# Attention scores and HGRN levels as matmuls of 64 rows for two heads, a layer norm tail with operands in PSUM, and another order of steps

## The chip, the cores and the metric

The kernel runs on one core of one Trainium2 chip. The metric is the device time of one execution in microseconds; a lower time is better. The engines are TensorE (PE), VectorE (DVE), ScalarE (ACT), GpSimd (POOL) and SyncE (SP), which issues most DMAs. PSUM is the memory that matmuls write to, in banks of 512 float32 per partition.

## What is computed

One layer on x of 512 tokens by 1024 features, float32. One projection gives all parts; three mixers work on them; their outputs, gated by silu, are projected back and normalised:

```python
h = x @ w_in[l]
...
o_nsa = nsa_mixer(...)               # 6 heads in 2 groups: compressed, selected and window branch
o_sb = stick_breaking_mixer(sb_q, sb_k, sb_v)                         # 4 heads
o_hg = hgrn2_mixer(hg_q, hg_f, hg_i, lb_all[l])                       # 6 heads
...
mixed = jnp.concatenate([o_nsa * jax.nn.silu(nsa_z), o_sb * jax.nn.silu(sb_z),
                         o_hg.astype(x.dtype) * jax.nn.silu(hg_z)], axis=-1)
x = layer_norm(ALPHA * x + (mixed @ w_out[l]).astype(x.dtype), ln_g[l], ln_b[l])
```

Heads are 64 wide. The scores of a head are its queries times its keys over these 64 features, for the selected and the window branch of the sparse attention (NSA, with a bias by distance) and for stick-breaking; the compressed branch does the same with 31 block keys. HGRN is a gated linear recurrence over time with a decay per feature: `att[t, s] = sum_d q[t,d] k[s,d] exp(b[t,d] - b[s,d])` within a chunk, and a carried state between chunks.

## The kernel before, in words

*Precision.* Operands of the large matmuls are split in two parts of a shorter float32 type (`F32R`): `hi`, a cast by ACT, and `lo`, the rest, by a subtraction on DVE, on POOL or through a DMA that adds (`split` L183, `load_part` from L262, with a choice for each weight group in `SPLITS`). A product takes three passes: hi with hi, hi with lo, lo with hi (`PASSES` L305).

*Projections.* For a group of weight columns, PE multiplies 8 pieces of 128 features with x. Results have the features on the partitions (`feat` L316 and `blocks` L329, 512 columns a matmul) or the tokens (`tiles` with `tok` L345, up to 274 columns). The out-projection is `out_part` (L902, 512 columns, and the addition to y on DVE at L903).

*Scores.* `qstack` (from L350) takes a block of two heads' queries and makes one tile a head, with hi in 64 of the 128 rows and lo in the other 64. `kstack` (from L360) makes two tiles a head: one with the keys' hi part in both halves, one with lo in the half that faces the queries' hi and zeros in the other. Two matmuls over 128 rows (`qk`, L377) then give all three passes for 128 queries by up to 512 keys. Stick-breaking (`sb_head`, from L685) calls it with 128, 256, 384 and 512 keys a head and adds scan, exponentials and a subtraction of its own on DVE and ACT (L696 to L704); the sparse heads (`nsa_probs`, from L652) with 256 keys for the first query tile (both branches at once), and with 256, 384 and 512 for the others, once a branch; `nsa_exp` (L648, L650) adds the bias, finds the extreme and exponentiates. `nsa_cmp` (from L610) uses 12 matmuls of 512 columns over the two groups (L617) for the compressed scores. `pv` (L384 to L402) transposes probabilities on PE and multiplies them with values.

*HGRN.* `hg_pair` (from L776) takes two heads at a time, 64 features each, so that both fill the 128 rows. The 512 tokens are 4 chunks of 128 (`NT`). Within a chunk the matrix `att` is built in 7 levels (`LEVELS`, 64 down to 1): at a level, a block's second half attends to its first half. DVE forms differences of decays, ACT exponentiates, DVE multiplies the queries by the result, one head at a time, into a tile `qz` in which each head's columns are zero in the other head's rows (L806, 64 rows by 256 elements). Four matmuls over 128 rows by 128 columns, in plain float32, make the level's values (L811), and a masked copy on DVE (L820) or copies on ACT (L817) put them into `att`. A matmul in plain float32 leaves two records on PE in the trace. After the levels come transposes and a product with a single output column (L835, L836), the state's products (L843) and the output's (L857, L859).

*Small matmuls of another shape.* `bias_tables` multiplies a one-hot matrix of 33 rows with a table of 6 columns (L473), for the bias by distance.

*The end.* For each of four token tiles `do_end` does the last part of the out-projection, then `norm_stats` (L905 to L922: statistics on DVE at L911 and L913, two small ACT operations at L915 and L916, the shift at L919 or L921) and `norm_apply` (L924 to L936). For tiles 0 to 2, ACT normalises, and DVE (where the tuple `LN_VECTOR` names it) or POOL multiplies by the weight `lng` (L934); POOL adds the bias `lnb` (L935). For tile 3, DVE does two operations that each combine two steps (L929, L930). The last half tile is projected in two pieces of 256 columns.

*What sets the order.* The string `ORDER` names steps one after the other; most steps are generators, and each mention advances one by one `yield`. So the program text is written in that order, and the scheduler of the tile framework places instructions on the engines in order of priority, which follows the program text unless `high_priority` is in force. `BUFS` gives buffers for the pools, `ENGINES` names the engine for some copies and products. An engine takes its instructions strictly in order, and semaphores tell it when an operand is there.

## Time and profile before

| what | value |
|---|---|
| median of 2 runs | 368.16 us (367.69 to 368.63) |
| the profiled execution's own time | 368.77 us |
| its span (first to last instruction) | 366.9 us |
| granted TensorE clock, mean over the span | 0.99 of full speed |
| busy: PE | 343.1 us (94%), 2002 instructions |
| busy: DVE | 276.8 us (75%) |
| busy: ACT | 248.1 us (68%) |
| busy: POOL | 103.8 us (28%) |

Busy time is time in which an engine works on at least one instruction. Weight loads (PEld) are a row of their own beside PE. The durations that the trace gives for single matmuls overlap with their neighbours', because matmuls are pipelined; the distance from one start to the next is the price. A chain of waits follows the end of the program back, at each step to what released the instruction.

### The profile page before, as it was taken

The numbers are of one execution on the slowest core, as the hardware profiler recorded it, in microseconds if no ns is written. First come the engines' busy times: TensorE is split into PE (matmuls) and PEld (weight loads), VectorE is DVE, ScalarE is ACT, GpSimd is POOL, SyncE is SP. The second block draws the span as 40 slices with busy tenths as digits, with TensorE's granted clock in tenths as the row PEclk, the third lists the DMA queues.
The fourth block names the chain that finished last, engine by engine and source line by source line (L and its number), as shares of the span: only waits on it lengthen the run. The fifth ranks groups of instructions, "written<-read, shape, count | busy, mean of one in ns | idle before, by whom it ended". The sixth has DMA issues, their size and how long they took to land.

```text
span 366.9 us, 5871 instructions
## 1 busy us (share of the span) xinstructions
PE 343.1 (94%) x2002; PEld 290.4 (79%) x2002; DVE 276.8 (75%) x628; ACT 248.1 (68%) x559; POOL 103.8 (28%) x145
## 2 busy tenths in 40 slices
PE   7999999999999998998999998999999899999980
PEld 5787899887888876876788997977877777888870
DVE  2769666689699888898876666788999657732796
ACT  3696963728559998785396777688889988731240
POOL 4065560001201111020471332242131604031092
PEclk9999999999999999999999999999999999999995
DMA  7767365250415472051348619500040698961023
GB/s 244 264 230 198 103 187 155 80 138 2 114 59 126 106 181 49 0 134 41 103 137 210 184 33 223 174 29 2 29 107 10 128 250 223 289 179 22 1 88 143
DMA packets 16910, 45.64 MB, mean 124 GB/s; under 512 B 2786, under 2 KB 3298, under 8 KB 16880
## 3 DMA queue, kind: packets, MB, share of 16 engines
q1 hardware_dynamic: 13568, 33.65, 27.5%
q0 software_dynamic: 3312, 11.61, 17.8%
q8 instruction: 16, 0.26, 0.3%
q14 instruction: 14, 0.11, 0.1%
HBM read 37.27 MB, written 2.14 MB: 107 GB/s over the span
## 4 chain that ended last, share of the span: by engine, by line
PE 56%; DVE 14%; ACT 11%; issue 10%; DMA 5%; POOL 3%; SPq 0%; DVEq 0%; POOLq 0%; ACTq 0%
PE pi L329 16%; PE pi L345 11%; PE pi L902 10%; PE pc L402 3%; PE ma L811 3%; DMA lo<-raw 3%; PE ma L377 2%; PE mb L395 2%; PE pi L316 2%; DVE sr L702 2%; DVE qz L806 2%; DMA xt<-xt 2%; ACT hi L273 2%; DVE att L820 1%; ACT pt L650 1%
## 5 line engine op out<-in xcount | busy, mean ns | idle before, releaser
L329 PE MATMUL pi<-xh,hi 128*128 128x512 f32 x160 | 47.8, 406 | 1.8 <-DVE vs L186 1.3
L329 PE MATMUL pi<-xh,lo 128*128 128x512 f32 x160 | 46.5, 396 | 1.4 <-DMA lo<-raw 1.4
L329 PE MATMUL pi<-xl,hi 128*128 128x512 f32 x160 | 46.6, 397 | 0.0
L902 PE MATMUL pi<-hi,mx 128*128 128x512 f32 (+1 forms) x134 | 40.9, 383 | 0.0
L329 PEld LDWEIGHTS pi<-xh,lo 128*128 128x128 f32 x160 | 29.3, 188 | 7.4 <-DMA lo<-raw 2.2
L329 PEld LDWEIGHTS pi<-xh,hi 128*128 128x128 f32 x160 | 28.5, 189 | 7.4 <-DVE vs L186 1.7
L329 PEld LDWEIGHTS pi<-xl,hi 128*128 128x128 f32 x160 | 29.3, 188 | 5.4
L186 DVE TENSOR_TENSOR pl<-mb,ph 128x384 fp32r<-128x384 f32 (+1 forms) x48 | 28.1, 595 | 6.8 <-ACT ph L185 6.3
L345 PE MATMUL pi<-lo,xh 128*128 128x256 f32 (+1 forms) x160 | 27.6, 286 | 1.5 <-DMA lo<-raw 1.3
L345 PE MATMUL pi<-hi,xh 128*128 128x256 f32 (+1 forms) x160 | 28.1, 290 | 0.6 <-DVE vs L186 0.6
L902 PEld LDWEIGHTS pi<-hi,mx 128*128 128x128 f32 x134 | 24.8, 188 | 4.5
L273 ACT CAST hi<-raw 128x1024 fp32r<-128x1024 f32 (+2 forms) x23 | 23.3, 1013 | 7.0 <-PE pi L902 2.8
L680 POOL TENSOR_SCALAR pt<-pt,sm,gates 128x256 f32<-128x256 f32 (+1 forms) x24 | 17.6, 740 | 33.5 <-DVE sm L677 29.3
L345 PE MATMUL pi<-hi,xl 128*128 128x256 f32 (+1 forms) x160 | 26.7, 284 | 0.0
L650 ACT ACTIVATE pt<-pt,mn 128x256 f32<-128x256 f32 (+3 forms) x42 | 24.5, 586 | 2.4 <-DVE mn L648 2.2
L902 PE MATMUL pi<-lo,mx 128*128 128x512 f32 (+1 forms) x67 | 25.8, 385 | 0.0
L185 ACT CAST ph<-mb 128x384 fp32r<-128x384 f32 (+1 forms) x48 | 24.0, 508 | 1.5 <-PE mb L395 1.3
L345 PEld LDWEIGHTS pi<-hi,xh 128*128 128x128 f32 x160 | 23.0, 190 | 1.6 <-DVE vs L186 0.8
L345 PEld LDWEIGHTS pi<-lo,xh 128*128 128x128 f32 x160 | 22.7, 191 | 1.9 <-DMA lo<-raw 1.5
L811 PEld LDWEIGHTS ma<-qz,kz 128*128 128x128 f32 x168 | 20.8, 191 | 3.7 <-ACT kz L795 1.1
L648 DVE CUSTOM_DVE_ANT_0 pt<-ma,nb 128x256 f32<-128x256 f32 (+3 forms) x42 | 21.2, 511 | 3.4 <-PE ma L377 3.3
L811 PE MATMUL ma<-qz,kz 128*128 128x128 f32 x168 | 22.7, 279 | 1.0 <-ACT kz L795 0.4
(269 smaller groups left out, 845.9 us busy)
## 6 DMA issues: line engine op xcount, KB each, us to landing
raw<-w_in SPq DMA_DIRECT2D x28, 512.0 KB, 3.6
lo<-raw POOLq DMA_DIRECT2D x9, 512.0 KB, 5.1
lo<-w_in POOLq DMA_DIRECT2D x6, 512.0 KB, 5.4
raw<-w_out SPq DMA_DIRECT2D x6, 512.0 KB, 5.1
lo<-w_out POOLq DMA_DIRECT2D x5, 512.0 KB, 5.4
y<-x SPq DMA_DIRECT2D x8, 256.0 KB, 4.2
out<-y SPq DMA_DIRECT2D x8, 256.0 KB, 2.0
xt<-xt SPq DMA_DIRECT2D x3, 512.0 KB, 7.2
```

What stands on the lines that cost most here:

```text
L185: nc.scalar.copy(hi, src)
L186: nc.vector.tensor_tensor(out=lo, in0=src, in1=hi.bitcast(F32), op=ALU.subtract)
L273: nc.scalar.copy(hi, raw)
L316: self.nc.tensor.matmul(ps, w[:, c0:c0 + P], self.xpart(x, kt), start=(n == 0 and j == 0), stop=(n == len(parts) - 1 and j == len(js) - 1))
L329: self.nc.tensor.matmul(ps, w[:, b * P:(b + 1) * P], self.xpart(x, kt), start=(n == 0 and j == 0), stop=(n == len(grp) - 1 and j == len(js ...
L345: self.nc.tensor.matmul(ps[:, :w_], self.xpart(x, kt)[:, i * P:(i + 1) * P], w[:, :w_], start=(j == 0), stop=(j == len(js) - 1))
L402: nc.tensor.matmul(acc[:, j * P:], vt[j], t[:, b:b + w], start=(first and j == 0 and t is h), stop=(last and j == 3 and t is l))
L648: nc.vector.tensor_tensor_reduce(out=dst, in0=src, in1=self.nb[h][:, n - 1::-1], scale=1.0, scalar=3e38, op0=ALU.add, op1=ALU.min, accum_o ...
L650: nc.scalar.activation(dst, dst, AF.Exp, bias=mn, scale=-1.0, accum_out=sm)
L680: (nc.gpsimd if i in POOL_TILES else nc.vector).tensor_scalar(out=pts[i], in0=pts[i], scalar1=sm[:, i:i + 1], scalar2=self.gates[:, i, c:c ...
L811: nc.tensor.matmul(ps[:, c * P:(c + 1) * P], kk[:, c * P:(c + 1) * P], qz[:, c, :, :].rearrange("p h t -> p (h t)"), start=True, stop=True)
L902: nc.tensor.matmul(ps, m, w[:, cs], start=(j == 0), stop=(j == len(jobs) - 1))
```

## The change

Scores. `pair` takes the place of `qstack` and `kstack`: it splits a block of two heads into one hi and one lo tile, each with the first head in rows 0 to 63 and the second in rows 64 to 127. `qk` issues three terms, each as one matmul over the upper 64 rows into one bank and one over the lower 64 rows into another bank. `sb_head` becomes `sb_pair` and `nsa_probs` takes a head of each group at once; `cmp_scores` does the compressed scores of both groups in 18 matmuls of 64 rows.

HGRN. The queries of both heads are multiplied in one full-height operation; the level's product is eight matmuls of 64 rows by 64 columns that alternate between the heads, each head in a bank of its own. `HG_STEPS` takes two levels in one step, with a PSUM tile of two banks for them (pool `psl`). The mask is stored four times over.

The end. Weight and bias of the layer norm are copied into PSUM by ACT, and DVE takes its operand from there; `LN_FORM` names engines by tile, half and operation. The statistics and the last application of tile 3 get `high_priority`, the application of tile 2 stands between them. `ORDER`, `BUFS`, `SPLITS` and `ENGINES` have new values.

```diff
 ORDER = (
-    "x Lhf1 Lhq 4*hf1 3*hq Lhi_sv 3*hi_sv Lhi hi_sv p1 hi Lsq hq hi p1 p0 hi 2*p1 const p1 hi 3*p1 sq p1 p0 sq 2*p0 "
...
+    "x Lhf1 4*hf1 3*hq Lhi_sv 2*hi_sv Lhq 2*hi_sv p1 hq Lsq p1 hi Lhi p0 hi const p1 2*sq hi p0 hi sq p1 p0 sk Lsk p0 "
...
-ENGINES = dict(cl='p', e20='v', e21='p', hq='a', hs='v', hv0='v', hv1='a', hv2='a', k1='a', kb0='v', kb1='v',
-    kb2='v', kd0='v', kt='v', mz0='v', mz1='v', mz2='p', mz3='v', mz4='v', nw0='v', nw1='v', nw2='v', q1='p', qs0='p',
-    qs1='p', qs2='p', tmpta='a', tmptb='v', ts='p', z0='v', z1='a', z2='a', z3='v')
+ENGINES = dict(cl='v', e20='v', e21='p', hq='a', hs='v', hv0='v', hv1='a', hv2='a', k1='a', kb0='v', kb1='p',
+    kb2='v', kd0='v', kt='v', mz0='v', mz1='v', mz2='v', mz3='v', mz4='p', nw0='v', nw1='v', nw2='v', q1='p', qs0='v',
+    qs1='p', qs2='v', tmpta='a', tmptb='v', ts='p', z0='v', z1='a', z2='a', z3='v')
...
+LN_FORM = (("pp", "vp"), ("pp", "pp"), ("vp", "vp"), ("s", "s"))
 WARM = 8
 LEVELS = (64, 32, 16, 8, 4, 2, 1)
 PLAIN = 32
+HG_STEPS = ((6, 0), (1, 2), (3, 4), (5,))
...
-    def qstack(self, ps, scale):
-        nc = self.nc
-        res = []
-        for b, o in ((0, 64), (64, 0)):
-            t = self.g2(dt=F32R, s="q")
-            hi, lo, src = t[b:b + 64, :], t[o:o + 64, :], ps[b:b + 64, :]
-            self.split(hi, lo, src, scale)
-            res.append(t)
...
-            self.zero_r(tl[o:o + 64, :], o)
-            src = ps[b:b + 64, :]
-            nc.scalar.copy(th[b:b + 64, :], src)
-            self.copy("kh", th[o:o + 64, :], src)
-            nc.vector.tensor_tensor(out=tl[b:b + 64, :], in0=src, in1=th[b:b + 64, :].bitcast(F32), op=ALU.subtract)
...
-    def qk(self, out, q, i, k):
-
-        lhs = q[:, i * P:(i + 1) * P]
-        for e in range(2):
-            self.nc.tensor.matmul(out, lhs, k[e], start=(e == 0), stop=(e == 1))
+    def pair(self, ps, scale=None, dst=None):
+        hi, lo = dst or (self.g2(dt=F32R, s="qh"), self.g2(dt=F32R, s="ql"))
+        self.split(hi, lo, ps, scale)
+        return hi, lo
+
+    HALVES = (slice(0, 64), slice(64, 128))
+    TERMS = ((0, 0), (0, 1), (1, 0))
+
+    def qk(self, outs, q, i, ks):
+
+        for n, (e, f) in enumerate(self.TERMS):
+            for out, r in zip(outs, self.HALVES):
+                self.nc.tensor.matmul(out, q[e][r, i * P:(i + 1) * P], ks[f][r], start=(n == 0), stop=(n == 2))
...
+    def cmp_scores(self):
...
+        jobs = [(hp, e, f) for e, f in self.TERMS for hp in range(HPG)]
+        for n, (hp, e, f) in enumerate(jobs):
+            for ps, r in zip(pss, self.HALVES):
+                nc.tensor.matmul(ps[0:96, :], self.kc[f][r, 64 - 32 * hp:160 - 32 * hp], self.q[hp][e][r],
+                                 start=(n == 0), stop=(n == len(jobs) - 1))
...
-            ps = self.ps()
-            self.qk(ps[:, :n], q, i, [t[:, branch, 0:n] for t in self.kk[g]])
-            self.nsa_exp(h, ps[:, :n], pts[i], mn[:, i:i + 1], sm[:, i:i + 1])
+            pss = [self.ps() for _ in heads]
+            self.qk([ps[:, :n] for ps in pss], q, i, ks(branch, n))
+            for h, ps, pts, (mn, sm) in zip(heads, pss, all_pts, stats):
+                self.nsa_exp(h, ps[:, :n], pts[i], mn[:, i:i + 1], sm[:, i:i + 1])
...
+            pss = [self.ps("mb") for _ in range(2)]
+            self.qk([ps[:, :n] for ps in pss], self.sq[p], i, [t[:, :n] for t in self.sk[p]])
...
-        for li in (6, *range(6)):
+        for ls in HG_STEPS:
+            ps = self.psl.tile([P, 2, S], F32, tag="ml", name=self.nm("ml"))
+            for n, li in enumerate(ls):
...
-            for h, r in heads:
-                qo = qz[r, :, h, :].rearrange("p c (n l) -> p c n l", l=L)
+                qv = q.rearrange("p (n l) -> p n l", l=2 * L)[:, :, L:2 * L]
+                qz = self.t2((P, 256), s="qz", tag="tq")
+                qo = qz.rearrange("p (n l) -> p n l", l=L)
...
-                    nc.vector.tensor_tensor(out=qo, in0=qv[r, :, :, 1, :], in1=evc[r, :, :, L:2 * L], op=ALU.mult)
+                    nc.scalar.activation(qz, qz, AF.Exp)
+                    nc.vector.tensor_tensor(out=qo, in0=qo, in1=qv, op=ALU.mult)
...
-            ps = self.ps()
-            for c in range(NT):
-                nc.tensor.matmul(ps[:, c * P:(c + 1) * P], kk[:, c * P:(c + 1) * P],
-                                 qz[:, c, :, :].rearrange("p h t -> p (h t)"), start=True, stop=True)
+                for c in range(NT):
+                    for h, r in heads:
+                        nc.tensor.matmul(ps[:, h, n * 256 + c * 64:n * 256 + c * 64 + 64], kk[r, c * P:(c + 1) * P],
+                                         qz[r, c * 64:(c + 1) * 64], start=True, stop=True)
+                pl = ps[:, :, n * 256:n * 256 + 256]
...
-                nc.vector.copy_predicated(att.rearrange("p c h (n k l) -> p (c h) n k l", k=2, l=L)[:, :, :, 1, :],
-                                          m.unsqueeze(1).to_broadcast([P, 8, 64 // L, L]),
-                                          ps.rearrange("p (g n l) -> p g n l", g=8, l=L))
+                    nc.vector.copy_predicated(att.rearrange("p h c (n k l) -> p h (c n) k l", k=2, l=L)[:, :, :, 1, :],
+                                              m.unsqueeze(1).to_broadcast([P, 2, 256 // L, L]),
+                                              pl.rearrange("p h (n l) -> p h n l", l=L))
...
+            m = LN_FORM[i][e]
+            if m == "s":
+                nc.vector.scalar_tensor_tensor(out=y[e], in0=y[e], scalar=nm, in1=self.lngp[e], op0=ALU.add, op1=ALU.mult)
+                nc.vector.scalar_tensor_tensor(out=y[e], in0=y[e], scalar=rs, in1=self.lnbp[e], op0=ALU.mult, op1=ALU.add)
             else:
                 nc.scalar.activation(y[e], y[e], AF.Identity, scale=rs, bias=nm)
-                eng = nc.vector if (i, e) in LN_VECTOR else nc.gpsimd
-                eng.tensor_tensor(out=y[e], in0=y[e], in1=self.lng[e], op=ALU.mult)
-                nc.gpsimd.tensor_tensor(out=y[e], in0=y[e], in1=self.lnb[e], op=ALU.add)
+                for f, g, gp, op in zip(m, (self.lng[e], self.lnb[e]), (self.lngp[e], self.lnbp[e]), (ALU.mult, ALU.add)):
+                    if f == "v":
+                        nc.vector.tensor_tensor(out=y[e], in0=y[e], in1=gp, op=op)
+                    else:
+                        nc.gpsimd.tensor_tensor(out=y[e], in0=y[e], in1=g, op=op)
...
+        self.lngp, self.lnbp = [], []
+        for l, lp in ((self.lng, self.lngp), (self.lnb, self.lnbp)):
+            for t in l:
+                lp.append(self.ps("mb"))
+                nc.scalar.copy(lp[-1], t)
...
-            st[i] = self.norm_stats(i)
-            if i:
+            if i == NT - 1:
+                with self.tc.high_priority():
+                    st[i] = self.norm_stats(i)
                 self.norm_apply(i - 1, *st[i - 1])
-        self.norm_apply(NT - 1, *st[NT - 1])
...
```

How the instructions move on the engines, in three places. The first is PE early in the projections, where HGRN levels stand between them. Before, a pair's levels stand as `L811` (four matmuls over 128 rows), here two levels behind the projection of `hi_574` and `lo_575` (names of the weight parts; `xh` and `xl` are the parts of x):

```order
L345 MATMUL pi_842<-hi_574,xh_128 128x256 x2
L345 MATMUL pi_842<-hi_574,xl_131 128x256 x2
L345 MATMUL pi_842<-hi_574,xl_132 128x256 x2
L345 MATMUL pi_842<-lo_575,xh_127 128x256 x2
L345 MATMUL pi_842<-lo_575,xh_128 128x256 x2
L811 MATMUL ma_876<-qz_390,kz_401 128x128 x4
L811 MATMUL ma_889<-qz_391,kz_402 128x128 x4
L835 MATMUL ma_904<-ident,kd_898 128x128 x3
```

Now each level is `L808`, eight matmuls of 64 rows and 64 columns, and pieces of a projection (`L331` is `blocks`, `L347` is `tok`) stand between levels:

```order
L331 MATMUL pi_461<-xh_133,lo_430 128x512 x2
L331 MATMUL pi_461<-xh_134,lo_430 128x512
L808 MATMUL ml_607<-qz_623,kz_402 128x64 x8
L331 MATMUL pi_461<-xh_134,lo_430 128x512
L808 MATMUL ml_663<-qz_666,kz_403 128x64 x8
L347 MATMUL pi_707<-hi_696,xh_131 128x256 x2
L347 MATMUL pi_707<-hi_696,xh_132 128x256 x2
L347 MATMUL pi_707<-hi_696,xl_135 128x256 x2
L347 MATMUL pi_707<-hi_696,xl_136 128x256
L808 MATMUL ml_663<-qz_682,kz_401 128x64 x8
```

Runs of 64-row matmuls now alternate with the projection's 128-row ones.

The second is PE in the scores of the sparse attention (`kk` are the keys' tiles, `q` or `qh`, `ql` the queries'). Before, two matmuls a query tile (`L377`), between pieces of a projection:

```order
L329 MATMUL pi_2948<-xh_126,hi_2935 128x512 x2
L329 MATMUL pi_2948<-xl_129,hi_2935 128x512
L377 MATMUL ma_2610<-kk_2085,q_1696 128x256
L377 MATMUL ma_2610<-kk_2086,q_1696 128x256
L377 MATMUL ma_2615<-kk_2085,q_1696 128x384
L377 MATMUL ma_2615<-kk_2086,q_1696 128x384
L329 MATMUL pi_2948<-xl_129,hi_2935 128x512
L329 MATMUL pi_2948<-xl_130,hi_2935 128x512
L377 MATMUL ma_2620<-kk_2085,q_1696 128x512
L377 MATMUL ma_2620<-kk_2086,q_1696 128x512
L377 MATMUL ma_2676<-kk_2085,q_1890 128x256
```

Now six matmuls for two heads (`L364`), the two banks in alternation:

```order
L347 MATMUL pi_2845<-hi_2753,xh_132 128x256
L347 MATMUL pi_2845<-hi_2753,xl_135 128x256 x2
L347 MATMUL pi_2845<-hi_2753,xl_136 128x256
L364 MATMUL ma_2665<-kk_2160,qh_1873 128x384
L364 MATMUL ma_2665<-kk_2161,qh_1873 128x384
L364 MATMUL ma_2665<-kk_2160,ql_1874 128x384
L364 MATMUL ma_2676<-kk_2160,qh_1873 128x512
L364 MATMUL ma_2677<-kk_2160,qh_1873 128x512
L364 MATMUL ma_2676<-kk_2161,qh_1873 128x512
L364 MATMUL ma_2677<-kk_2161,qh_1873 128x512
```

Here, too, a run of 64-row matmuls follows 128-row ones of a projection (`L347`).

The third is DVE at the very end (`y` are the output tiles, `ln` the weights of the norm). Before, the two multiplications of tile 2 (`L934`) stand behind the last addition of a matmul (`L903`) or between it and the last statistics (`L911`):

```order
L921 TENSOR_SCALAR nm_4039<-mv_4034,rs_4036 128x1
L911 BN_STATS bn_4082<-y_3777 128x6
L903 SCALAR_TENSOR_TENSOR y_3873<-y_3873,pi_4060 128x256
L911 BN_STATS bn_4082<-y_3777 128x6
L911 BN_STATS bn_4082<-y_3873 128x6
L903 SCALAR_TENSOR_TENSOR y_3873<-y_3873,pi_4071 128x256
L934 TENSOR_TENSOR y_3758<-y_3758,ln_3892 128x512
L911 BN_STATS bn_4082<-y_3873 128x6
L934 TENSOR_TENSOR y_3854<-y_3854,ln_3894 128x512
L913 BN_AGGR mv_4087<-bn_4082 128x2
L919 TENSOR_SCALAR nm_4092<-mv_4087 128x1
L929 SCALAR_TENSOR_TENSOR y_3777<-y_3777,nm_4092,ln_3892 128x512
```

Now the addition is `L901`, the statistics `L909` and `L911`, and the operands `mb` of the multiplications and of the last operations (`L928`, `L929`) are the copies in PSUM:

```order
L919 TENSOR_SCALAR nm_4161<-mv_4156,rs_4158 128x1
L909 BN_STATS bn_4204<-y_3948 128x6 x2
L901 SCALAR_TENSOR_TENSOR y_3986<-y_3986,pi_4182 128x256
L934 TENSOR_TENSOR y_3872<-y_3872,mb_4013 128x512
L909 BN_STATS bn_4204<-y_3986 128x6
L901 SCALAR_TENSOR_TENSOR y_3986<-y_3986,pi_4193 128x256
L934 TENSOR_TENSOR y_3967<-y_3967,mb_4015 128x512
L909 BN_STATS bn_4204<-y_3986 128x6
L911 BN_AGGR mv_4209<-bn_4204 128x2
L917 TENSOR_SCALAR nm_4214<-mv_4209 128x1
L928 SCALAR_TENSOR_TENSOR y_3948<-y_3948,nm_4214,mb_4013 128x512
L928 SCALAR_TENSOR_TENSOR y_3986<-y_3986,nm_4214,mb_4015 128x512
```

One multiplication and one statistic stand ahead of the last addition.

## Rows read from the trace of the kernel before

**Rows 1.** The page's first part: the span, and TensorE, VectorE, ScalarE, GpSimd.

```profile
span 366.9 us, 5871 instructions
...
PE 343.1 (94%) x2002; PEld 290.4 (79%) x2002; DVE 276.8 (75%) x628; ACT 248.1 (68%) x559; POOL 103.8 (28%) x145
```

**Rows 2.** Busy time by stage: each engine's us (count), PE clock, DMA share, GB/s.

```profile
70.00:170.00 100.00, 94.98 (x574) 80.29 (x573) 87.24 (x188) 73.06 (x170) 13.46 (x21) 1.00 0.38 94
70.00:320.00 250.00, 239.70 (x1435) 201.96 (x1434) 201.95 (x498) 189.56 (x449) 59.94 (x84) 1.00 0.44 115
320.00:356.50 36.50, 36.43 (x170) 30.34 (x168) 20.48 (x37) 12.11 (x21) 12.97 (x11) 1.00 0.29 79
356.50:367.00 10.50, 0.00 (x0) 0.00 (x0) 7.32 (x10) 0.68 (x3) 3.60 (x3) 0.63 0.34 126
```

**Rows 3.** Chain of waits, whole span: its shares by line.

```profile
PE pi L329 16%; PE pi L345 11%; PE pi L902 10%; PE pc L402 3%; PE ma L811 3%; DMA lo<-raw 3%; PE ma L377 2%; PE mb L395 2%; PE pi L316 2%; DVE sr L702 2%; DVE qz L806 2%; DMA xt<-xt 2%; ACT hi L273 2%; DVE att L820 1%; ACT pt L650 1%
```

**Rows 4.** Chain of waits, pieces on PE: start us, us, engine, line.

```profile
18.43 16.32 PE pi L329 x72
...
44.07 8.83 PE pi L345 x72
...
52.90 0.89 PE ma L811 x8
```

**Rows 5.** Timeline of PE, 76.8 to 78.1 us: start us, us, engine, line, operation.

```profile
76.85 0.55 PE L859 MATMUL ma<-hv,att 128*128 128x64 f32 x4
77.23 0.44 PE L857 MATMUL ma<-st,qs 128*128 128x128 f32 x2
77.51 0.56 PE L859 MATMUL ma<-hv,att 128*128 128x64 f32 x4
```

**Rows 6.** Timeline of PE, 33.9 to 35.8 us.

```profile
33.91 0.84 PE L329 MATMUL pi<-xh,lo 128*128 128x512 f32 x3
34.68 0.45 PE L473 MATMUL mb<-one,tb 33*6 33x512 f32 x2
35.05 0.73 PE L329 MATMUL pi<-xh,hi 128*128 128x512 f32 x2
```

**Rows 7.** Groups by line and form: busy us, mean ns of one, idle before.

```profile
L806 DVE TENSOR_TENSOR qz<-hq,e 64x256 f32<-64x256 f32 x36 | 15.7, 436 | 0.5
...
L189 DVE SCALAR_TENSOR_TENSOR q<-pi,q 64x512 fp32r<-64x512 f32 x10 | 6.9, 688 | 0.3
...
L367 ACT CAST kh<-pi 64x512 fp32r<-64x512 f32 x4 | 2.3, 581 | 2.1 <-DVE kl L369 1.6 <-PE pi L329 0.5
```

**Rows 8.** Chain of waits, pieces of query and key casts.

```profile
84.47 0.68 DVE q L189
...
127.11 0.69 DVE kl L369
```

**Rows 9.** Timeline of the tail, 352 to 364 us (VectorE and GpSimd).

```profile
352.28 0.69 DVE L903 SCALAR_TENSOR_TENSOR y<-y,pi 128x512 f32<-128x512 f32 x1 [0.28 <-PE pi L902]
352.33 1.29 POOL L934 TENSOR_TENSOR y<-y,ln 128x512 f32<-128x512 f32 x1 [0.18 <-ACT y L932]
...
355.39 0.42 DVE L903 SCALAR_TENSOR_TENSOR y<-y,pi 128x256 f32<-128x256 f32 x1
...
356.47 0.42 DVE L903 SCALAR_TENSOR_TENSOR y<-y,pi 128x256 f32<-128x256 f32 x1
356.81 1.32 DVE L934 TENSOR_TENSOR y<-y,ln 128x512 f32<-128x512 f32 x1
...
358.39 1.63 DVE L934 TENSOR_TENSOR y<-y,ln 128x512 f32<-128x512 f32 x1
359.94 0.25 DVE L913 BATCH_NORM_AGGREGATE mv<-bn 128x2 f32<-128x24 f32 x1
...
360.41 2.16 DVE L929 SCALAR_TENSOR_TENSOR y<-y,nm,ln 128x512 f32<-128x512 f32 x2
362.49 1.40 DVE L930 SCALAR_TENSOR_TENSOR y<-y,rs,ln 128x512 f32<-128x512 f32 x2
```

More of the change, by code (lines that the diff above doesn't have):

```diff
@@ L114, in constants @@
                  & ((s[:, None] % (2 * L) < L) | ((s[:, None] % (2 * L) == L) & (s[:, None] == t[None, :]))))
-    c["hgmask"] = np.concatenate(m, 1).astype(np.float32)
+    c["hgmask"] = np.concatenate([np.tile(t, (1, NT)) for t in m], 1).astype(np.float32)
     return c
@@ L607, in comp_v @@
             self.vcz.append(z)
+    def cmp_scores(self):
+        nc = self.nc
+        cbs, pss = [self.cmp_bias(g) for g in range(2)], [self.ps() for _ in range(2)]
+        jobs = [(hp, e, f) for e, f in self.TERMS for hp in range(HPG)]
[3 more added lines that the diff above has]
+                                 start=(n == 0), stop=(n == len(jobs) - 1))
+        self.cst = []
+        for ps, cb in zip(pss, cbs):
+            st = self.t2((96, S), s="st", tag="ta")
+            nc.vector.tensor_tensor(out=st, in0=ps[0:96, :], in1=cb, op=ALU.add)
+            self.cst.append(st)
     def nsa_cmp(self, g):
         nc = self.nc
-        cb = self.cmp_bias(g)
-        ps = self.ps()
-        for hp in range(HPG):
-            for e in range(2):
-                nc.tensor.matmul(ps[0:96, :], self.kc[g][:, e, 64 - 32 * hp:160 - 32 * hp], self.q[hp][g], start=(hp == 0 and e == 0),
-                                 stop=(hp == 2 and e == 1))
-        st = self.t2((96, S), s="st", tag="ta")
-        nc.vector.tensor_tensor(out=st, in0=ps[0:96, :], in1=cb, op=ALU.add)
+        st = self.cst[g]
         ps = self.ps()
@@ L705, in sb_head @@
             if i < NT - 1:
                 yield
-        self.sb[h] = a
+        for e in range(2):
+            self.sb[2 * p + e] = both[e]
     def hg_lower(self):
@@ L814, in hg_pair @@
[L814 to L822 removed]
+                    nc.vector.tensor_tensor(out=qo, in0=bv[:, :, L:2 * L], in1=bv[:, :, L:L + 1].to_broadcast([P, nb, L]),
+                                            op=ALU.subtract)
@@ new lines, in hg_pair @@
+                if L >= PLAIN:
+                    for r in range(0, P, 2 * L):
+                        rows = slice(r, r + L + 1)
+                        nc.scalar.copy(att[rows, :, :, r + L:r + 2 * L],
+                                       pl[rows].rearrange("p h (c l) -> p h c l", c=NT)[:, :, :, r // 2:r // 2 + L])
+                else:
+                    m = self.hgmask[:, li * 256:(li + 1) * 256].rearrange("p (n l) -> p n l", l=L)
+                    nc.vector.copy_predicated(att.rearrange("p h c (n k l) -> p h (c n) k l", k=2, l=L)[:, :, :, 1, :],
+                                              m.unsqueeze(1).to_broadcast([P, 2, 256 // L, L]),
+                                              pl.rearrange("p h (n l) -> p h n l", l=L))
@@ L1070, in keys @@
         if not self.kk:
-            self.kk = [[self.room(self.kkp, "kk", 1024, (P, 2, S), F32R, "kk") for _ in range(2)] for _ in range(2)]
-        self.kstack(ps, [[t[:, branch] for t in ts] for ts in self.kk])
+            self.kk = [self.room(self.kkp, "kk", 1024, (P, 2, S), F32R, "kk") for _ in range(2)]
+        self.pair(ps, dst=[t[:, branch] for t in self.kk])
     def do_vc_ks(self):
```

211 lines of the change are left out of this document (97 added, 114 removed), and 11 rows, old and new, of the table ORDER.

## Prediction

> **What bounds the kernel now.** I read the first part of the page, then the busy time by stage, then the chain of waits, then single stretches of TensorE and of the end. The page has TensorE (PE) busy for 343.1 of 366.9 us and VectorE (DVE) for 276.8 [rows 1]. By stage, PE is busy for 95.0 of 100 us between 70 and 170 us, where DVE has 87.2, for 239.7 of 250 us between 70 and 320, and without a gap from 320 to the last matmul at 356.4; after that there are 10.5 us in which PE does nothing [rows 2]. So what PE must do comes first, and DVE beside it in the stage of 70 to 170. The chain of waits agrees: its three largest entries are the PE lines of the projections, 16, 11 and 10% of the span, and the largest of DVE have 2% [rows 3].
>
> A busy PE is a stream whose price per matmul can be read. 72 matmuls of 512 columns take 16.32 us, 0.227 each; 72 of 256 columns 8.83 us, 0.12 each; 8 records of a level (128 columns, float32, two records per matmul) 0.89 us, 0.112 each [rows 4]. I put 384 columns at 0.175, between their neighbours. Narrow float32 matmuls are not cheaper: four records of 64 columns and two of 128 columns repeat every 0.66 us (76.85, 77.51), which is again 0.112 for each of the six [rows 5]. Every record brings its own load of 128 weight columns, and below 128 moving columns that load sets the pace.
>
> **The change part by part.** *Scores.* Before, a head costs two 128-row passes: the stick-breaking heads (4) 2 x (0.112 + 0.12 + 0.175 + 0.227) = 1.27 each, 5.1 us; the sparse-attention heads (6) 2 x (0.12 + 2 x 0.522) = 2.33 each, 14.0; the compressed scores 12 x 0.227 = 2.7; together 21.8. After, two heads cost three pairs of 64-row passes. If the two of a pair run beside each other, a pair costs what one costs now: 2 x 3 x 0.634 = 3.8, plus 3 x 3 x (2 x 0.112 + 2 x 0.522) = 11.4, plus 9 x 0.227 = 2.0; together 17.2, so -4.6. If they run one behind the other it is +12.7. No row of before has two such matmuls, so both ends stand. I take -4.6: upper and lower half use different rows of the array and different PSUM banks, nothing in the program makes them wait for each other, and almost all of them alternate.
>
> *Levels.* 21 levels of 8 records are 21 x 8 x 0.112 = 18.8 us. After, there are 16 records a level, of 64 columns, each still with a load of 128 columns. Beside each other that is 8 slots of 0.112: no gain at all, in spite of half the columns. One behind the other it is 37.6, +18.8. I take 0, with the same argument.
>
> *Entering and leaving the half height.* At 34 us PE goes from 128-row matmuls to one of 33 rows and 6 columns and back. Three matmuls begin at 33.91 and should have handed over at 34.59; the next begins at 34.68. Its two (0.227, and 0.06 for 128 columns, half the price of 256) should have ended at 34.97; PE goes on at 35.05, and the second matmul from there begins at 35.39 (its end at 35.78 less its 0.39), 0.34 behind the first instead of 0.227 [rows 6]. That is 0.09 + 0.08 + 0.11 = 0.285 us for one excursion, with no wait for data in it. The changed program has 56 runs of 64-row matmuls between 128-row ones, where the program before has three such excursions and three to a single output column, which stay: 56 x 0.285 = 16.0. Bounds: nothing, if a change of height alone does not stop the stream (the row seen changes the width too), and 56 x 0.4 = 22, if the first load of a run, now of 128 columns, is unhidden as well. I take 16.0, the row itself. Nearly every run begins with a semaphore wait; PE now idles 10 us between 70 and 320 [rows 2], and an excursion that falls into such a wait is free: -4, between 0 and -10. The Trainium skill (TensorEngine Tiling (Array Packing), Tiling Modes) says the same of the cause: changing the tiling mode, not just the tile, drains TensorE, and it lists 64x128 as a mode of its own. The trace agrees for the modes it has, at 0.285 us; by that rule 16 us are owed, without it none.
>
> *Vector and scalar work.* The 36 half-height products at 436 ns become 18 of full height at some 0.42 (-8.2 us of DVE), ten low parts of queries at 688 ns become five (-3.4), and the casts of keys, 16 of 0.58 us on ACT (four such groups of four), become four (-7) [rows 7]; the eight subtractions of keys, 0.69 each [rows 8], become four (-2.8). Work that moves from GpSimd to DVE gives some 5 of these 14.4 back. How much reaches the end I read from the chain: the products are 2% of it, 7 us [rows 3], of which half goes; of its pieces on query and key casts (0.7 us each, some nine of them) about half goes too [rows 8]. Together -7. Bounds: 0, if the PE stream, which is 95% busy there, was the limit all along, and -14, all that is removed.
>
> *Tail.* Last add of a matmul at 356.47, end of the last DVE instruction at 362.49 + 1.40 = 363.9. Between them two multiplications take 1.32 and 1.63 us while GpSimd works, and two more operations 2.16 [rows 9]. With one operand in PSUM a DVE operation takes 0.69 even while GpSimd runs (352.28 beside 352.33). Priority puts a multiplication and a statistic ahead of the last add, so from the end of the first half's add (355.39 + 0.42 = 355.8) the chain is 0.69 + 0.34 (half-width adds and statistics hand over after 0.34, 356.47 to 356.81) + 0.34 + 0.69 + 0.34 + 0.47 (359.94 to 360.41) + 4 x 0.69 = 5.6: end at 361.4, -2.5. I take -2.0, since ten pieces will not follow each other without a gap. Bounds 0 and -3.4. The four copies into PSUM (some 0.6 us each) stand in ACT's queue ahead of the last weight casts and wait for the loads of the norm's weights; ACT is busy 12 of 36.5 us there and PE has over 20 us of matmuls queued before it needs those casts [rows 2], so nothing; with that cover gone, 2 us.
>
> *Other order.* The table reorders all stages; nothing in the trace prices that, 0 with 4 us either way.
>
> **Sum.** -4.6 + 0 + 16.0 - 4 - 7 - 2.0 + 0 = -1.6 us, against the profiled execution of 368.77 us (1.9 around its span of 366.9), which lies 0.6 above the median of 368.16. From the median: 366.6 us. With excursions between 0.2 and 0.4, relief between -2 and -14 and the order's 4 us, this case lies between 357 and 376.
>
> **Rivals.** *Half height costs no stop.* If only a change of width stops the stream, the 16.0 and the -4 fall away: -4.6 - 7 - 2.0 = -13.6, 354.6 us. For it: every excursion seen changes the width. Against it: a full-height matmul needs all rows, so it must wait for both halves.
>
> *Weights are loaded one half after the other (slower).* The place is PE's weight loads: 0.112 a load [rows 5]. Two halves whose matmuls overlap but whose loads queue pay 0.22 a pair up to 384 columns: scores 23.3 instead of 17.2, levels +18.8. From the sum, +6.1 + 18.8 = +24.9, so 391.5 us, or 379.5 without the stops. It decides as soon as the loads of a pair take over 0.15 us together. For it: the loads are what bounds narrow matmuls now. Against it: two halves fill different rows. The Trainium skill (TensorE: Matmul & The Clock Gate, LDWEIGHTS) has a load's time follow its columns and not its rows; so half the rows would save nothing in a load, and this rival stands or falls with whether two loads overlap, which no run here shows.
>
> *Nothing overlaps,* so that the change does not do what it says: scores +12.7 instead of -4.6, levels +18.8, 402.7 us. For it only that the trace never shows two matmuls at once; against it the separate banks and rows.
>
> **How the numbers follow.** Overlap with stops 0.44, overlap without stops 0.31, loads in turn 0.16, nothing overlaps 0.09. About 2%, 7.4 us, is what a measurement of this kernel can tell from no change: 360.8 to 375.5. Faster: 0.29 of the second case and 0.09 of the first, 0.38. Slower: 0.23 of the last two and 0.09 of the first, 0.32. The rest, 0.30. The range reaches from the second case less its order term (351) to loads in turn with stops (391); left out are the last case and half of the third's upper side.
>
> **What would show it.** Right: pairs of 64-row matmuls begin a few ns apart, a level takes 0.9 us, each run costs some 0.3 us at its ends, the multiplications after the last matmul take 0.69. Wrong: a level of 1.8 us (loads in turn), or a 128-row matmul that follows a run within its usual 0.12 to 0.23 us (no stop). PE's gaps between 70 and 170 us growing would say that the order, not PE, sets the end.

## The result and the profile after

The changed kernel takes 385.38 us (385.23 to 385.54) where the kernel before takes 368.16: ratio 1.047, interval 1.041 to 1.053. It is slower by 17.2 us; the forecast was 366.6 us, 1.6 us faster.

First the busy time by stage of the kernel after (columns as in [rows 2]):

```profile
70.00:170.00 100.00, 95.88 (x718) 80.31 (x717) 75.79 (x168) 68.03 (x163) 6.57 (x10) 1.00 0.41 100
70.00:320.00 250.00, 241.65 (x1589) 196.29 (x1588) 184.05 (x469) 167.67 (x412) 45.65 (x67) 0.99 0.35 90
280.00:310.00 30.00, 29.89 (x167) 22.64 (x166) 20.32 (x61) 19.42 (x52) 7.41 (x9) 1.00 0.00 1
320.00:372.50 52.50, 48.19 (x215) 39.28 (x214) 25.27 (x41) 22.51 (x38) 13.63 (x12) 0.97 0.52 140
```

Between 70 and 320 us DVE works 184.1 us where it worked 202.0, ACT 167.7 where it worked 189.6 [rows 2]. PE's idle time there goes from 10.3 to 8.4 us: 40 us less work on the two engines, 2 us less idling of PE. In the same stretch PE does less of the program. And from 280 to 310 us the DMA engines carry nothing.

The timeline of PE around one level, the counterpart of the excursion in [rows 6]:

```profile
51.26 0.64 PE L347 MATMUL pi<-lo,xh 128*128 128x256 f32 x4
51.83 1.11 PE L808 MATMUL ml<-qz,kz 64*128 64x64 f32 x16
52.87 0.50 PE L331 MATMUL pi<-xl,hi 128*128 128x512 f32 x1
53.20 0.63 PE L331 MATMUL pi<-xh,lo 128*128 128x512 f32 x2
```

The fourth of the four matmuls that begin at 51.26 should hand over at 51.74; the level begins at 51.83, 0.09 late. Its 16 records are eight pairs, whose two matmuls begin, by the start times in the trace, within 8 ns of each other: at 0.112 a pair they should end at 52.73. The next matmul begins at 52.87, 0.14 late (0.05 of it because the second pair's load comes late, 0.09 at the exit), and the second matmul behind it 0.33 after the first in place of 0.227. Together 0.335 us for one visit to the half height, with no wait in it.

The tail of the kernel after, DVE's timeline (compare [rows 9]):

```profile
374.28 0.68 DVE L934 TENSOR_TENSOR y<-y,mb 128x512 f32<-128x512 f32 x1
...
375.21 0.40 DVE L901 SCALAR_TENSOR_TENSOR y<-y,pi 128x256 f32<-128x256 f32 x1
375.53 0.68 DVE L934 TENSOR_TENSOR y<-y,mb 128x512 f32<-128x512 f32 x1
...
378.39 1.40 DVE L929 SCALAR_TENSOR_TENSOR y<-y,rs,mb 128x512 f32<-128x512 f32 x2
```

The multiplications take 0.68 where they took 1.32 and 1.63, and from the start of the last addition to the end of the last operation it is 4.6 us (375.21 to 379.79) where it was 7.4.

What is new stands in the views of waits of the kernel after. PE's longest (engine, line, for whom: us in total, times, longest):

```profile
PE pi L900 <- DMA lo<-raw: 2.7, 1, 2.7
PE pi L900 <- DMA lo<-w_out: 1.6, 1, 1.6
```

And the longest of SP's queue, in the same columns:

```profile
SPq L890 <- PE mb L382: 51.6, 1, 51.6
```

At the start of the out-projection (`L900`) PE waits 4.3 us for low parts of weights. SP's queue stood for 51.6 us, until 311 us, behind one load of y (`L890`) that waited for a transpose of the last probabilities. That is the stretch without DMA above. In the kernel before the same 30 us carry 171 GB/s:

```profile
280.00:310.00 30.00, 28.59 (x152) 22.68 (x151) 20.72 (x56) 27.06 (x58) 9.45 (x12) 1.00 0.69 171
```

The stand of the queue is not what PE waits for. The rows on these weights in the kernel after are, from the load to the wait (`L275` is ACT's cast; the two groups on POOL issue the DMAs that make low parts, with the count and the first and last start; the last line has the time from issue to landing of these three):

```profile
258.83 0.81 SPq L271 DMA_DIRECT2D raw<-w_out  x2
...
317.04 1.07 ACT L275 CAST hi<-raw 128x1024 fp32r<-128x1024 f32 x1
...
L278 POOL DMA_DIRECT2D lo<-w_out x2: 867/880/892, 319.7 to 324.9; - x2
L280 POOL DMA_DIRECT2D lo<-raw x1: 862/862/862, 321.9 to 321.9; - x1
...
DMA to landing us min/median/max: 5.4/9.2/9.4
...
325.14 0.50 PE L900 MATMUL pi<-lo,mx 128*128 128x512 f32 x1 [1.57 <-DMA lo<-w_out]
...
331.13 0.61 PE L900 MATMUL pi<-lo,mx 128*128 128x512 f32 x1 [2.74 <-DMA lo<-raw]
```

The next load of output weights after the two at 258.83 is issued at 321.66, so what ACT casts from 317 to 321 was loaded ahead of the stand. The casts come 6 us ahead of the first use at 322.86 (16 us in the kernel before, 288.9 for 304.5), and two of the low parts then take a DMA: issued at 319.7, landed 5.4 us later, and issued at 321.9, landed 9.2 us later, which is when PE's two waits end.

### The profile page after: what moved, and what is told of

Read it like the earlier page. It is cut to its first block, busy times and chain, and to the rows that moved or that the text cites. A ratio compares the mean times of both kernels' runs of the same rounds, so it can differ in the third digit from the quotient of the medians.

```text
span 383.1 us, 6296 instructions
## 1 busy us (share of the span) xinstructions
PE 359.8 (94%) x2252; PEld 295.6 (77%) x2252; DVE 263.9 (69%) x610; ACT 237.6 (62%) x543; POOL 89.9 (23%) x125
## 5 line engine op out<-in xcount | busy, mean ns | idle before, releaser
L331 PE MATMUL pi<-xh,hi 128*128 128x512 f32 x160 | 46.8, 403 | 0.0
L331 PE MATMUL pi<-xl,hi 128*128 128x512 f32 x160 | 46.3, 397 | 0.0
L331 PE MATMUL pi<-xh,lo 128*128 128x512 f32 x160 | 45.2, 394 | 0.0
L900 PE MATMUL pi<-hi,mx 128*128 128x512 f32 (+1 forms) x134 | 41.0, 389 | 0.0
L188 DVE TENSOR_TENSOR pl<-mb,ph 128x384 fp32r<-128x384 f32 (+1 forms) x48 | 28.2, 597 | 12.6 <-ACT ph L187 12.3
L331 PEld LDWEIGHTS pi<-xh,lo 128*128 128x128 f32 x160 | 29.8, 188 | 6.4 <-issue 0.5
L331 PEld LDWEIGHTS pi<-xl,hi 128*128 128x128 f32 x160 | 29.5, 188 | 6.1
L331 PEld LDWEIGHTS pi<-xh,hi 128*128 128x128 f32 x160 | 28.7, 188 | 5.8 <-issue 0.5
L644 ACT ACTIVATE pt<-pt,mn 128x256 f32<-128x256 f32 (+3 forms) x42 | 24.3, 580 | 10.3 <-DVE mn L642 10.3
L900 PE MATMUL pi<-lo,mx 128*128 128x512 f32 (+1 forms) x67 | 25.9, 391 | 4.3 <-DMA lo<-raw 2.7
L347 PE MATMUL pi<-hi,xh 128*128 128x256 f32 (+1 forms) x160 | 28.5, 292 | 1.3 <-DVE si L418 1.3
L900 PEld LDWEIGHTS pi<-hi,mx 128*128 128x128 f32 x134 | 25.3, 192 | 5.0 <-DVE mx L188 0.2
L347 PE MATMUL pi<-lo,xh 128*128 128x256 f32 (+1 forms) x160 | 28.2, 287 | 0.0
L347 PE MATMUL pi<-hi,xl 128*128 128x256 f32 (+1 forms) x160 | 28.2, 288 | 0.0
L285 ACT CAST hi<-raw 128x1024 fp32r<-128x1024 f32 (+2 forms) x21 | 20.9, 997 | 8.7 <-PE pi L331 4.0
L808 PE MATMUL ml<-qz,kz 64*128 64x64 f32 x336 | 23.4, 277 | 2.8 <-DVE att L818 1.5
L808 PEld LDWEIGHTS ml<-qz,kz 64*128 64x128 f32 x336 | 20.6, 187 | 6.8 <-DVE att L818 2.7
L347 PEld LDWEIGHTS pi<-hi,xh 128*128 128x128 f32 x160 | 22.7, 190 | 3.5 <-issue 2.3
L901 DVE SCALAR_TENSOR_TENSOR y<-y,pi 128x512 f32<-128x512 f32 (+1 forms) x17 | 11.0, 653 | 19.4 <-PE pi L900 19.4
```

Of the source, the lines that this page charges most:

```text
L188: nc.vector.tensor_tensor(out=lo, in0=src, in1=hi.bitcast(F32), op=ALU.subtract)
L285: nc.scalar.copy(hi, raw)
L331: self.nc.tensor.matmul(ps, w[:, b * P:(b + 1) * P], self.xpart(x, kt), start=(n == 0 and j == 0), stop=(n == len(grp) - 1 and j == len(js ...
L347: self.nc.tensor.matmul(ps[:, :w_], self.xpart(x, kt)[:, i * P:(i + 1) * P], w[:, :w_], start=(j == 0), stop=(j == len(js) - 1))
L644: nc.scalar.activation(dst, dst, AF.Exp, bias=mn, scale=-1.0, accum_out=sm)
L808: nc.tensor.matmul(ps[:, h, n * 256 + c * 64:n * 256 + c * 64 + 64], kk[r, c * P:(c + 1) * P], qz[r, c * 64:(c + 1) * 64], start=True, sto ...
```

## The experiments

Theory A: each run of 64-row matmuls between 128-row ones costs 0.285 us and a little more, and this is most of the loss. Theory B: the stops fall into waits, and the new order costs the time. Runs 7 to 11 add theory C: what the order costs is the stall ahead of the out-projection. The kernel before ran beside each set, at 368.9 us; that is the time to compare with.

**1. Levels at 128 rows.**

```diff
-                    for h, r in heads:
-                        nc.tensor.matmul(ps[:, h, n * 256 + c * 64:n * 256 + c * 64 + 64], kk[r, c * P:(c + 1) * P],
-                                         qz[r, c * 64:(c + 1) * 64], start=True, stop=True)
+                    h, w = c % 2, c // 2 * P
+                    nc.tensor.matmul(ps[:, h, n * 256 + w:n * 256 + w + P], kk[:, c * P:(c + 1) * P], qz[:, w:w + P],
+                                     start=True, stop=True)
```

> The changed kernel with the HGRN levels as four matmuls of 128 rows by 128 columns again, over both heads' rows at once (it leaves out keeping the two heads apart, so the levels' values are mixed); everything else, the full-height products too, as in the changed kernel. Theory A (each run of 64-row matmuls costs PE 0.285 us at its ends and some 0.05 for the second load of its first pair): 20 runs go, 20 x 0.335 = 6.7 us, and a level's own price stays at some 0.9 us: 378.7 us. Theory B (the new order and its waits cost the time, stops fall into waits anyway): 385 us, within 1.5.

Measured: 385.4 us (382.3 to 386.8), as theory B has it. But the windows show something that neither theory has, a fall of the granted clock (the third number from the right):

```profile
252.00:256.00 4.00, 3.33 (x19) 2.62 (x20) 2.60 (x8) 2.22 (x7) 2.94 (x5) 0.81 0.64 121
256.00:260.00 4.00, 4.00 (x18) 2.81 (x16) 2.25 (x13) 3.06 (x12) 0.00 (x0) 0.50 0.59 133
260.00:264.00 4.00, 4.00 (x9) 1.57 (x7) 2.26 (x7) 2.04 (x7) 0.00 (x0) 0.50 0.31 120
264.00:268.00 4.00, 4.00 (x17) 2.83 (x17) 0.82 (x4) 1.07 (x5) 1.31 (x2) 0.50 0.00 0
268.00:272.00 4.00, 4.00 (x17) 2.94 (x17) 3.56 (x12) 3.44 (x10) 0.69 (x2) 0.56 0.00 0
```

After a gap of 0.85 us near 252 (the changed kernel has one as long at 253) PE runs at 1.2 GHz until about 271 us. Against the full clock that is 4 x (0.19 + 3 x 0.50 + 0.44) = 8.5 us of work lost, more than the 6.7 that were to be gained. The four executions of the run point the same way: 386.7 and 386.8 us at a mean clock of 0.97, 384.1 at 0.986, 382.3 at 0.990. Inconclusive by itself; run 9 repeats it.

**2. Scores at 128 rows.**

```diff
-        for n, (e, f) in enumerate(self.TERMS):
-            for out, r in zip(outs, self.HALVES):
-                self.nc.tensor.matmul(out, q[e][r, i * P:(i + 1) * P], ks[f][r], start=(n == 0), stop=(n == 2))
+        for out in outs:
+            for n, (e, f) in enumerate(self.TERMS[:2]):
+                self.nc.tensor.matmul(out, q[e][:, i * P:(i + 1) * P], ks[f], start=(n == 0), stop=(n == 1))
```

(the compressed scores likewise)

> The changed kernel with the scores as two matmuls of 128 rows per head again, on the tiles of the changed kernel (it leaves out the third term and keeping the two heads apart); levels of 64 rows, casts and order stay. Theory A: 38 runs go, 38 x 0.335 = 12.7 us, and the pace of four full-height matmuls in place of three pairs costs 4.6 again: 385.4 - 8.1 = 377.3 us. Theory B: nothing returns and the 4.6 are paid: 390 us.

Measured: 380.3 us (379.4 to 381.1). The sign is theory A's, the size 5.1 of the 8.1 us. What is missing stands in the trace: PE's own work falls by some 8 us, but PE waits 1.5 us longer in all (4.8 us at one place in the out-projection, 4.3 at two in the kernel after), and the lower clock takes 1.7 us more (it falls near 131, 149 and 323 us; the table below has the sums).

**3. Both at 128 rows:** the two edits together.

> Both edits together, no 64-row matmul left in the changed kernel (leaves out the same as the two above). Theory A: -6.7 - 8.1 = -14.8 us, 370.6 us, and the first order's 2.0 us of the tail stay gained, so what lies above 366.2 is the order's. Theory B: 390 us.

Measured: 376.6 us (375.3 to 378.0), 8.8 less than the changed kernel and 7.7 more than before. So without any 64-row matmul the changed kernel is still slower: theory A accounts for a part and does not suffice.

**4. Prices one by one.**

```diff
+        for n in (512, 384, 256):
+            for _ in range(12):
+                mm(pa, full, n)
+            for _ in range(12):
+                mm(pa, top, n)
+                mm(pb, bot, n)
+            for _ in range(12):
+                mm(pa, top, n)
...
```

> The kernel before with dummy matmuls on zeros ahead of its work, for prices one by one: 12 of 128 rows, then 12 pairs of 64 rows in alternation, then 12 of the upper half alone, at 512, 384 and 256 columns; eight excursions of two pairs of 64 rows between two of 128 rows; eight excursions to 32 output columns at full height; float32 levels of either form; only the trace is read. Theory A: a pair costs what one costs (0.227, 0.175, 0.12), the upper half alone costs the same for each, an excursion to 64 rows 0.285 to 0.335 us. The excursion to 32 output columns: 0.285 too if any change of shape stops the stream, 0 if only the height counts. If overlap fails for wide ones (B's neighbour): a pair at 512 columns 0.45 us.

Read by windows that hold one sequence each (us, then PE's busy time and its matmuls, one of them the neighbour's): 12 pairs at 512 columns, 12 of the upper half alone, eight excursions in height, eight in width, eight float32 matmuls of a level as before, and as after.

```profile
7.20:10.07 2.87, 2.87 (x25) 2.35 (x25) 1.41 (x2) 2.13 (x3) 0.00 (x0) 1.00 0.94 354
10.08:12.57 2.49, 2.49 (x13) 2.02 (x11) 2.38 (x4) 2.05 (x4) 0.00 (x0) 1.00 0.50 136
24.21:34.82 10.61, 10.61 (x49) 4.76 (x48) 0.00 (x0) 0.00 (x0) 0.00 (x0) 1.00 0.24 77
35.16:42.32 7.16, 7.16 (x32) 4.54 (x31) 0.00 (x0) 0.00 (x0) 0.00 (x0) 1.00 0.00 0
42.32:44.19 1.87, 1.87 (x17) 1.75 (x15) 0.00 (x0) 0.00 (x0) 0.00 (x0) 1.00 0.00 0
44.19:46.12 1.93, 1.93 (x33) 1.86 (x33) 0.00 (x0) 0.00 (x0) 0.00 (x0) 1.00 0.00 0
```

A pair costs 2.87 / 12 = 0.239, the late second load included, 0.23 without; the upper half alone 2.49 / 11 = 0.226: a half-height matmul is not cheaper, but its partner is free, its weight load too. An excursion in height takes 10.61 / 8 = 1.326 for four slots of 0.227: 0.418 us lost, 0.09 at each end and 0.11 for the second slot on each side. An excursion to 32 output columns: 31 matmuls in 7.16, 0.231 each, nothing lost. So it is the height alone that stops the stream, and the excursion of [rows 6], in which height and width change, was the height's.

**5. The stops added to the kernel before.**

```diff
+                    r = slice(0, 64 if j in (3, 8) else P)
-                    self.nc.tensor.matmul(ps, w[:, b * P:(b + 1) * P], self.xpart(x, kt), start=(n == 0 and j == 0),
+                    self.nc.tensor.matmul(ps, w[r, b * P:(b + 1) * P], self.xpart(x, kt)[r], start=(n == 0 and j == 0),
```

> The kernel before, unchanged in order, buffers and engines, but in each twelve matmuls of a projection with 512 columns two (never neighbours) run over the upper 64 rows alone (it leaves out 64 features of those products). The number of matmuls and their columns stay, so do all loads: 40 x 2 = 80 runs of one 64-row matmul are added. Theory A (a change between 128 and 64 rows stops PE: 0.09 in, 0.09 out, 0.105 for the second matmul behind it): 80 x 0.285 = 22.8 us, of which a part falls into waits that are there anyway: 386 to 392 us. Theory B (stops are free or hidden, the new order costs): 369 to 372 us.

Measured: 389.75 us (389.5 to 390.1), +20.8, or 0.26 us a visit, with order, loads and matmul count of the kernel before. The time lies in theory A's range, but by luck: the price was too low and the share that shows too high. By the start times a visit costs 0.40 us at its place: the first, at 19.36, begins 0.318 after the matmul ahead of it, the next one 0.428 later and the one behind that 0.334 later, 0.09, 0.20 and 0.11 more than 0.227. That is 32 us for 80 visits, of which two thirds show; PE's idle time falls from 11.5 to 4.3 us. Theory B as the whole cause is refuted.

**6. The tail alone, on the kernel before.** The edit is the last part of the change (`norm_apply`, `do_end`, `LN_FORM`).

> The kernel before with the new layer norm tail alone (copies in PSUM, engines by tile, priority and order of the last statistics and applications). Both theories: -2.0 us as in the sum, 366.9 us beside 368.9; 368.9 if the tail gives nothing.

Measured: 365.96 us (365.2 to 366.6), ratio 0.9916 (0.9897 to 0.9936): -3.0 us. It is faster than both kernels, and the best of all runs.

**7. Weights ahead of y and their low parts on DVE, on the changed kernel.**

```diff
-        ws = {kt: self.out_weights(kt, 2, half) for kt in (6, 4)}
-        mid = {3: self.out_weights(3, 1, half)}
+        if half == 0:
+            self.ow = [({kt: self.out_weights(kt, 2, e) for kt in (6, 4)}, {3: self.out_weights(3, 1, e)}) for e in range(2)]
+        ws, mid = self.ow[half]
```

(and `o3`, `o4`, `o6` of `SPLITS` as `(1, 1)`: low parts by a subtraction on DVE)

> The changed kernel, with the weights of both halves of the out-projection loaded ahead of the first load of y on SP's queue, and their low parts made on DVE instead of by a DMA. Theory C (the new order's cost is the stall before the out-projection: 4.6 us of waits and some 1.5 us at the lower clock behind them): 385.4 - 6 = 379.4 us. If the order's cost is spread over the stages: 384 to 385.5 us.

Measured: 379.9 us (379.2 to 380.7), -5.5, near theory C. PE has no wait for weights in the out-projection any more. But the queue of SP still stands, now behind a load of weights, and the stretch without DMA is the same:

```profile
SPq L271 <- DVE lo L287: 83.2, 8, 61.3
...
280.00:310.00 30.00, 29.92 (x169) 22.72 (x169) 21.16 (x62) 19.44 (x52) 6.06 (x7) 1.00 0.00 1
```

Four loads of output weights are issued ahead of the stand, as in the changed kernel, and ACT casts them as late (from 318.3); what differs is that the low parts come from DVE, in 1.2 us or less each from 319.9 on, and are there when PE begins at 324.1. So the traces put the gain down to the low parts on DVE and not to the order of the loads; no run has one without the other.

**8. Both at 128 rows, with the early weights.**

> The changed kernel without any 64-row matmul in scores and levels (leaves out what the two single edits left out) and with the early weights: measured 376.6 us without the early weights. Theory C: its wait of 4.8 us and the lower clock behind it go, -6 to -7.5: 369 to 370.5 us, the time of the kernel before. If the order's cost is spread: 375 us or more.

Measured: 372.1 us (369.0 to 374.5 in ten executions), -4.5 where theory C has -6 to -7.5. Beside run 6 (366.0) some 6 us of the new order remain. PE's waits in this run stand in many places:

```profile
PE ml L808 <- DVE att L818: 2.8, 5, 0.9
PE pi L318 <- ACT hi L187: 2.1, 1, 2.1
PE mb L567 <- DMA w<-w_ck: 2.0, 1, 2.0
PE pi L331 <- DVE vs L188: 1.8, 1, 1.8
```

**9. Run 1 again, with the early weights.**

> The run with early weights (379.9 us) with the HGRN levels at 128 rows as in the first run (it leaves out keeping the two heads apart there). Theory A, with the part of the stops that showed so far (13 of 18 us): 20 x 0.34 x 0.7 = 4.8 us less, 375.1 us. If the first run's 385.4 us came from the levels themselves and not from the lower clock that its trace shows from 255 to 272 us: 380 us or more. If the lower clock at that place comes again, up to 8 us stand on top, and the windows show it.

Measured: 376.9 us (376.2 to 377.1), -3.0 beside run 7, and its trace has the full clock from 8 us to the last matmul. Run 7's has not: it loses 3.4 us (near 13 and 259 us) to the lower clock, so most of the -3.0 can be the clock's. Of the profiled executions, run 9's is 4.5 us shorter than run 7's with 3.4 us less lost to the clock, and run 1's is 1.4 us longer than the changed kernel's with 6.8 us more lost. So the levels' stops are worth some 1 to 5 us at the end, and run 1 lost that to the clock; that the gap at 252 made the clock fall is only argued.

**10. Run 2 again, with the early weights.**

> The run with early weights (379.9 us) with the scores at 128 rows as in the second run (it leaves out the third term and keeping the heads apart). Theory A: 38 runs go, of which 70% show, 38 x 0.34 x 0.7 = -9.0, and the pace costs 4.6 again; the lower clock near 256 us goes too, some -1: 374.5 us. If the scores' stops are hidden: 384 us.

Measured: 374.6 us (373.7 to 375.7), as theory A has it. But the forecast took the lower clock near 256 us away, and the trace has it near 132 and 151 us instead, 5.1 us lost. Runs 9 and 10 add up, -3.0 - 5.4 = -8.4, and both edits together (run 8) give -7.8; as run 9 lost less to the clock than run 7 and run 10 more, that is in part luck.

**11. Fewer runs of levels, with the early weights.**

```diff
+                made.append((kk, qz))
+            for n, (kk, qz) in enumerate(made):
                 for c in range(NT):
...
```

> The run with early weights (379.9 us) with the matmuls of the two levels of a step issued one after the other, everything computed as in the changed kernel: some 11 runs of levels where 20 were. Theory A: 9 x 0.34 x 0.7 = -2.1, 377.8 us. If the number of runs does not matter, or both levels now wait for the later one: 380 us or more.

Measured: 375.35 us (374.2 to 376.6), -4.6 beside run 7, twice the forecast. The trace has 49 runs of 64-row matmuls where there were 58. Of the 5.3 us between the two profiled executions PE's idle time makes 2.9, the lower clock 1.7, and PE's own work the rest; which waits became shorter was not taken apart.

## Why the prediction was wrong, step by step

One table for what follows, of the profiled executions (us): when the last matmul begins, and where PE's time from 8 us to there goes. Lost to the clock is half of the time at 1.2 GHz; work is the rest of the busy time. Waits that are too short to leave PE idle count as work, so its differences are good to a few us.

| run | execution | last matmul | idle | lost to the clock | work |
|---|---|---|---|---|---|
| before | 368.8 | 356.2 | 11.5 | 0.0 | 336.7 |
| 6, tail alone | 366.4 | 356.2 | 11.3 | 0.0 | 336.9 |
| 5, visits added | 389.8 | 377.3 | 4.3 | 0.0 | 365.0 |
| changed kernel | 385.2 | 374.4 | 13.2 | 3.4 | 349.8 |
| 1, levels full | 386.7 | 375.8 | 12.3 | 10.2 | 345.3 |
| 2, scores full | 379.9 | 369.1 | 14.7 | 5.1 | 341.3 |
| 3, both full | 378.0 | 367.1 | 17.7 | 3.4 | 338.0 |
| 7, early weights | 380.7 | 370.2 | 11.4 | 3.4 | 347.4 |
| 8, early, both full | 373.8 | 363.3 | 15.3 | 1.7 | 338.3 |
| 9, early, levels full | 376.2 | 365.7 | 9.9 | 0.0 | 347.8 |
| 10, early, scores full | 375.7 | 365.2 | 10.4 | 5.1 | 341.7 |
| 11, early, batched | 375.4 | 364.9 | 8.5 | 1.7 | 346.7 |

The runs split the loss in three, beside 368.9 us: the tail -3.0 (run 6); the new order with its buffers, engines and casts, without 64-row matmuls, 376.6 - 366.0 = +10.6 (runs 3 and 6); the half height 385.4 - 376.6 = +8.8 (run 3). By the same parts the forecast had -2.0, then -7 + 0, then -4.6 + 0 + 16.0 - 4 = +7.4.

- **Half height: mechanism right, the price too low.** Pairs overlap, so the two rivals without overlap fall, and so does the one without a stop. By the matmul prices run 3's scores are 5.7 us dearer on PE than the changed kernel's (an estimate: the forecast 4.6 and 1.1 for first query tiles taken in two halves), so the stops are worth 8.8 + 5.7 = 14.5 us at the end; both traces lose 3.4 us to the clock. On PE they are worth some 17.5 (work 349.8 - 338.0, and 5.7). Forecast: 16.0 for 56, 12 of them visible. The row that it took, 0.285 for an excursion, is under what undisturbed visits cost: 0.335 for a level, 0.40 for one matmul of 512 columns (run 5), 0.418 for two pairs (run 4). What was missing is the second slot of a visit, 0.05 late for levels and 0.11 at 512 columns, which was named as a bound only (56 x 0.4 = 22). A level costs 0.95 before its exit, 0.90 in the forecast.
- **Tail: right.** -3.0 for -2.0, inside the bounds; the ten pieces do follow each other nearly without a gap.
- **"Vector and scalar work ... together -7": the step that failed first.** It read the chain: 2% are products, so half of 7 us must come back. But a chain names, for each moment, who came last, and when that one is quicker another can come just behind (this is argued, not shown). PE was idle for 10.3 of the 250 us [rows 2], and that was all that relief could give back. Nothing of it shows: with the relief and without 64-row matmuls PE idles longer than in run 6 (17.7 us in run 3 and 15.3 in run 8, against 11.3), and the 8.4 of the changed kernel stand beside visits that fill waits, as in run 5. The bound that stood beside it, 0 "if the PE stream was the limit all along", fits.
- **"Other order ... 0 with 4 us either way": the step that failed by most.** It took the absence of a row for a price of zero. Of the 10.6 us, 4.5 to 5.5 are the stall ahead of the out-projection (runs 7 and 8), the clock behind it included: low parts that a DMA makes, from casts that come 6 us ahead of their use. For the 6 that are left the profiled executions of runs 8 and 6, 7.4 us apart, give the parts: 4.0 us are waits of PE, for mask copies, casts and a load, 1.7 the lower clock near 148 us, and 1.4 work, about what the first query tiles in two halves cost by the estimate above. Which of the new values of `ORDER`, `BUFS`, `SPLITS` and `ENGINES` brings these waits was not taken apart. Relief and order were not separated: both are in the 10.6.
- **The cover of the four copies into PSUM** held: run 6 has them, and gains.

The Trainium skill (TensorEngine Tiling (Array Packing), Tiling Modes) puts the stop on every change of the tiling mode; the runs agree for 128 against 64 rows (0.418 us, run 4), while 32 output columns in place of 128 at full height cost nothing; that list has 128x32 as another mode, but the trace gives only active rows and columns, so whether these matmuls were in it is not shown. The same section says that different tiles can load weights and multiply in parallel; run 4 agrees: a pair of a level, with two loads, goes by in 1.93 / 16 = 0.12 where one record with its load takes 1.87 / 16 = 0.117 (each window ends with one stop; by the start times both are 0.112).

So 8.8 us came by the mechanism that the prediction had right (+7.4 by its own terms), and 10.6 from the part that it had at -7. The time lies inside the range (351 to 391), but not by its mechanism: the range reaches that far up only for weights loaded in turn, which run 4 rules out, and the case that held ended at 376.

## What to carry to other kernels

Price a change of matmul height by its visits: 0.33 to 0.42 us each where nothing else holds PE, whatever is done in there (runs 4 and 5); two half-height matmuls cost what one does, so a visit has to save more than that (here 58 visits saved an estimated 5.7 us and cost some 17.5), and 32 output columns in place of 128 were free. Work removed from engines that feed a busy PE gives back at most PE's idle time in that stage, whatever share the chain of waits gives it. When steps are reordered, look at how long ahead of its use each operand is begun and by what it is made: a low part took 5.4 to 9.4 us by DMA and 1.2 on DVE. A long stand of a DMA queue (51.6 us here) is no price by itself: run 7 has a longer one and no wait of PE for weights.
